# Attention weights turned on VectorE and through DRAM instead of on TensorE, in a fused encoder layer

## The chip, the cores and the metric

The kernel runs on one core of a Trainium2 chip. The metric is the time of one execution on the device, in microseconds (us). Three runs of the kernel before took 1556.53, 1554.85 and 1553.82 us: the median is 1554.85. Five engines run instructions side by side, each in the fixed order of its own queue: TensorE (PE, with its weight load PEld) multiplies matrices and transposes, VectorE (DVE), ScalarE (ACT) and GpSimd (POOL) do elementwise work, and SyncE (SP) issues DMAs. ScalarE issues some DMAs too.

## The reference, cut to what matters

One residual layer of an encoder for 1024 positions (S) of width 1024 (D), all in float32:

```python
h = rmsnorm(x, g_mix)
z = h @ w_in                                  # pooling channels | q | k | v
y_pool = pool_mixer(z[:, :512])               # windows of 2, 4, 8, 16
# per head (8), two maps i (head dimension 64), values of width 128:
s_i = qn_i @ kn_i.T - slope * |dist|          # masked to chunks of 64
a   = softmax(s_0) - lam * softmax(s_1)
o   = head_rmsnorm(a @ v) * 0.8
gates  = sigmoid(h @ w_gate + b_gate)
merged = gates[:, :D] * (y_pool @ w_bp) + gates[:, D:] * (o @ w_ba)
x = x + merged @ w_out
x = x + square(relu(rmsnorm(x, g_ffn) @ w_up)) @ w_down
```

What matters here is `a @ v`: TensorE sums over the partition axis, so it needs `a` with the keys on the partitions, while the scores come out with the queries there. The weights have to be turned in between.

## The kernel before, in words

**Precision.** Every large product is made from float32 operands split into a rounded part hi and a rest lo. `split` (L115) makes hi with a ScalarE cast (L117) and lo with a subtraction on VectorE or GpSimd (L118); `mm3` (L120) issues three products (L123 to L125).

**Stages.** First come input norm, the projections of q, k and v, attention, and beside it the projections for gates and pooling; then the branch projections (tiles bp, ba), the output projection, and the two halves of the MLP. The change touches only the first stage. The 1024 queries are cut into 8 blocks t of 128, so a head has 8 steps and attention has 64 steps g = 8h + t.

**The steps of attention.** `stage` (L620) gives for each letter a generator. A (`stage_qkv`, L418): one z tile of 384 columns, 24 products. B (`stage_prep`, L430): norms of q and k, from a sum of squares (L436, L437), a power on GpSimd (L249) and a product on VectorE (L441); splits v. C (`stage_qkT`, L453): two TensorE transposes of q and k into a PSUM tile tk (L459), then six ScalarE casts and six VectorE subtractions on half tiles of 64 x 128 (L468 to L473) into K and Q. D (`stage_scores`, L477): products of scores, t + 1 key blocks wide (L499, L500), the distance penalty and row minimum on VectorE (L502), the exponential on ScalarE (L510), and the combination of the two maps on VectorE (L519); the result, s, lies with the queries on the partitions. E (`stage_aT`, L545): transposes of each 128 x 128 block of s on TensorE into a PSUM tile ta (L555), up to four at a time, split into AT tiles. F (`stage_pv`, L565), for each pair p of query blocks: 6 (p + 1) products of V with AT, 256 columns wide (tile po). H and R sum squares for the output norm. W loads the next head's weights.

**Order.** A loop over g issues, at step g, the letter with offset n for item g - n; the offsets stand in one string, and offsets between letters say by how many steps a later letter trails. The gate and pool projections are made by `gates` and `pool_group` (L700 to L757), 40 units in all, a unit being 24 products of 512 columns (tiles g and u), their weights loaded on SP (L671) and split on ScalarE and GpSimd. In the text they stand behind the whole of attention. The text's order gives priorities: a scheduler lays each engine's queue out ahead of the run, taking at each moment of its own simulated time the ready instruction that comes first in the text. So the gate units, though last in the text, lie between attention's instructions wherever TensorE would otherwise have stood.

**Buffers.** K (two tiles), V (two), s (one tile for t < 4, two otherwise), AT (1, 2, 3 and 4 tiles for the four pairs) and some early tiles all come from one pool U of eleven buffers of 4 KB per partition; a tile takes a free buffer and gives it back after its last reader. z has two PSUM banks, tk and ta share two, the fillers have one.

```python
O = "B1 C2 H6 D3 R7 E4 F5 W-2 A0"
ORDER = [(w[0], int(w[1:])) for w in O.split()]
N_U, N_W, N_RAW, N_V = 11, 8, 2, 6
```

Of the kernel before, what the change touches and what calls it, by code (L numbers as in the profile page):

```python
# [8 lines left out]
F32 = mybir.dt.float32  # L9
# [25 lines left out]
N_Q, N_QN = 3, 2  # L35
N_Z, N_S, N_T, N_F = 2, 2, 2, 1
N_YU = 5
# [10 lines left out]
O = "B1 C2 H6 D3 R7 E4 F5 W-2 A0"  # L48
ORDER = [(w[0], int(w[1:])) for w in O.split()]
G_FIRST, G_Z = 13, 13  # L50

# [4 lines left out]
def encoder_kernel(  # L56
# [187 lines left out]
    yd = dram.tile([S, D], F32, name="yd")  # L244

# [41 lines left out]


    with ExitStack() as ph:
        sp = ph.enter_context(tc.tile_pool(name="sp", bufs=1))  # L290
        ps_s = ph.enter_context(tc.tile_pool(name="ps_s", bufs=N_S, space=PSUM))
        ps_o = ph.enter_context(tc.tile_pool(name="ps_o", bufs=1, space=PSUM))
        ps_t = ph.enter_context(tc.tile_pool(name="ps_t", bufs=N_T, space=PSUM))

        def s1(shape, dt, name, tag, bufs=1):
            return sp.tile(shape, dt, tag=tag, name=name, bufs=bufs)

        xs = {}

        def utf(shape, name):  # L300
            return ut(shape, F32, name)

        def kv_tiles(h):
            K = [ut([P, 2, 512], F32R, f"K{h}_{i}") for i in range(2)]
            V = [ut([P, 4, 2, P], F32R, f"V{h}_{i}") for i in range(2)]
            KV[h] = (K, V)

        def load_x(t):
            xs[t] = ut([P, D], F32, f"x{t}")
            for c in range(0, D, 512 if t == 0 else D):  # L310
                e = c + 512 if t == 0 else D
                nc.sync.dma_start(xs[t][:, c:e], x[t * P : (t + 1) * P, c:e])

        w_qkv = w_in[:, POOLD:].rearrange("(kk p) (s c) -> p kk s c", p=P, s=3)
        Wh = {}

        raws = {}

        def load_w(h, kp, raw_fn=raw):
            rw = raw_fn([P, 2, 384], f"rqkv{h}_{kp}")  # L320
            for i in range(2):
                nc.sync.dma_start(
                    rw[:, i, :].rearrange("p (s c) -> p s c", s=3),
                    w_qkv[:, 2 * kp + i, :, h * P : (h + 1) * P],
                )
            raws[h, kp] = rw

        def norm_x(t):
            if t % 4 == 0:
                hT.update(alloc_T(htile, "hT", t // 4))  # L330
            if FU >> t & 1:
                hn = fu_tile(f"hn{t}")
            else:
                hn = ut([P, D], F32, f"hn{t}")
            banks = [(ps_t, "tr"), (ps_s, "sc")][: 2 if t < N_SC else 1]
            norm_transpose(xs.pop(t), gmb, t, hT, hn, sp, banks, t == 0)

        def split_w(h, kp, eng):
            rw = raws.pop((h, kp))
            for i in range(2):  # L340
                w = wt([P, 2, 384], f"wqkv{h}_{2 * kp + i}")
                split(w[:, 0, :], w[:, 1, :], rw[:, i, :], eng)
                Wh.setdefault(h, []).append(w)

        KV = {}
        hT = {}
        for w in START.split():
            if w[0] == "x":
                load_x(int(w[1]))
            elif w[0] == "n":  # L350
                norm_x(int(w[1]))
            elif w[0] == "w":
                load_w(0, int(w[1]), utf if w[2:] else raw)
            elif w[0] == "s":
                split_w(0, int(w[1]), nc.gpsimd if w[2:] else nc.vector)
            elif w[0] == "g":
                gmb = ut([P, D], F32, "gmb")
                nc.sync.dma_start(gmb, g_mix[0].partition_broadcast(P))


        rows = sp.tile([32, P], F32, name="rows")
        nc.gpsimd.memset(rows, 0.0)
        nc.sync.dma_start(rows[0:16, :], b_gate[0].rearrange("(r p) -> r p", p=P))
        nc.sync.dma_start(rows[16:20, :], pool_scale[0].rearrange("(r p) -> r p", p=P))
        nc.sync.dma_start(rows[20:21, :], g_sub)

        gqk = sp.tile([P, 2, HD], F32, name="gqk")
        nc.sync.dma_start(gqk[:, 0, :], g_q[0].partition_broadcast(P))
        nc.sync.dma_start(gqk[:, 1, :], g_k[0].partition_broadcast(P))
        lqk = s1([P, 4, HD], F32, "lqk", "oq")  # L370
        nc.sync.dma_start(lqk, lambda_qk[0].partition_broadcast(P))

        dist = sp.tile([P, S], F32, name="dist")

        def distances():

            di = ut([P, S], I32, "di")
            nc.gpsimd.iota(di, pattern=[[-1, S]], base=S - P, channel_multiplier=1)
            nc.scalar.activation(dist, di, AF.Abs)
            nc.gpsimd.memset(dist[0:64, S - 64 : S], MASKED)  # L380

        def columns():
            cols_ps = ps_t.tile([P, 512], F32, tag="tr", name="cols_ps")
            nc.tensor.transpose(cols_ps[:, 0:32], rows, identf[0:32, 0:32])
# [17 lines left out]
        nlam = sp.tile([P, 1], F32, name="nlam")  # L402

        st = {}
        ATs = {}
        Zs = {}
        SS = {}

# [915 lines left out]
```

## Time and profile before

| | |
|---|---|
| median of the three runs | 1554.85 us |
| span of the profiled execution, first to last instruction | 1551.6 us |
| median of the runs above that span | 3.2 us |
| instructions | 22088 |
| TensorE clock granted | 1.000 |
| packets and bytes of DMA | 168009, 206.94 MB |

The profile is of one execution. An engine's busy time is the time in which at least one of its instructions runs; TensorE's instructions overlap, so that the sum of a group's durations and the group's busy time differ. A row of a group gives line, engine, operation, the tiles written and read (buffer numbers left out), the shape, the count, then the busy time in us and the mean duration of one in ns, then the idle time of the engine before these instructions with what ended it. A row of the timeline gives start, duration and the instruction. A row of the waits gives who waited for whom, us in total, times, and the longest. A row of DMA issues gives count, size of one, and the median us from issue to landing. "SPq" is the queue of SyncE.

### The profile page before, as it was taken

The numbers are of one execution on the slowest core, as the hardware profiler recorded it, in microseconds if no ns is written. First come the engines' busy times: TensorE is split into PE (matmuls) and PEld (weight loads), VectorE is DVE, ScalarE is ACT, GpSimd is POOL, SyncE is SP. The second block draws the span as 40 slices with busy tenths as digits, with TensorE's granted clock in tenths as the row PEclk, the third lists the DMA queues.
The fourth block names the chain that finished last, engine by engine and source line by source line (L and its number), as shares of the span: only waits on it lengthen the run. The fifth ranks groups of instructions, "written<-read, shape, count | busy, mean of one in ns | idle before, by whom it ended". The sixth has DMA issues, their size and how long they took to land.

```text
span 1551.6 us, 22088 instructions
## 1 busy us (share of the span) xinstructions
PE 1533.6 (99%) x7649; PEld 1320.8 (85%) x7649; DVE 1011.3 (65%) x2277; ACT 816.7 (53%) x1810; POOL 354.8 (23%) x449
## 2 busy tenths in 40 slices
PE   7999999999999999999999999999999999999999
PEld 6999999999998989888888887888888788888887
DVE  7777677777878787746422458866665667556662
ACT  6656556656566555645532547565555633333331
POOL 5433334243525262324363400000000000000000
PEclk9999999999999999999999999999999999999999
DMA  7111212021202031248536534554343799437650
GB/s 229 51 53 48 66 41 68 24 75 37 75 28 83 28 96 42 69 147 284 179 122 210 168 112 124 182 185 155 129 142 109 278 334 370 170 122 257 224 190 27
DMA packets 168009, 206.94 MB, mean 133 GB/s; under 512 B 10117, under 2 KB 104026, under 8 KB 167898
## 3 DMA queue, kind: packets, MB, share of 16 engines
q1 hardware_dynamic: 150490, 178.23, 35.0%
q10 hardware_dynamic: 17408, 27.30, 4.7%
q8 instruction: 60, 0.98, 0.3%
q14 instruction: 51, 0.42, 0.1%
HBM read 150.94 MB, written 54.56 MB: 132 GB/s over the span
## 4 chain that ended last, share of the span: by engine, by line
PE 89%; DVE 4%; DMA 3%; ACT 1%; issue 1%; POOL 1%; SPq 0%; ACTq 0%; POOLq 0%; DVEq 0%
PE z L125 5%; PE z L123 5%; PE z L124 5%; PE Da L124 4%; PE Da L123 4%; PE Da L125 4%; PE g L123 3%; PE g L124 3%; PE g L125 3%; PE Db L124 3%; PE Db L123 3%; PE Db L125 3%; PE X L125 2%; PE X L123 2%; PE X L124 2%; PE sc L499 2%
## 5 line engine op out<-in xcount | busy, mean ns | idle before, releaser
L123 PE MATMUL z<-wqkv,hT 128*128 128x384 f32 x512 | 174.7, 342 | 0.4 <-DVE qn L441 0.3
L125 PE MATMUL z<-wqkv,hT 128*128 128x384 f32 x512 | 174.3, 341 | 0.5 <-DVE hT L118 0.5
L124 PE MATMUL z<-wqkv,hT 128*128 128x384 f32 x512 | 173.8, 339 | 0.0
L510 ACT ACTIVATE s<-s,nm 128x256 f32<-128x256 f32 (+7 forms) x128 | 99.6, 778 | 49.2 <-DVE nm L502 44.1
L249 POOL TENSOR_TENSOR ms<-ms,mhalf 128x4 f32<-128x4 f32 x64 | 66.6, 1040 | 157.7 <-DVE ms L248 139.1
L125 PE MATMUL g<-hT,fwgate 128*128 128x512 f32 x256 | 101.0, 394 | 0.0
L124 PE MATMUL g<-hT,fwgate 128*128 128x512 f32 x256 | 100.9, 394 | 0.0
L123 PE MATMUL g<-hT,fwgate 128*128 128x512 f32 x256 | 100.9, 395 | 0.0
L123 PEld LDWEIGHTS z<-wqkv,hT 128*128 128x128 f32 x512 | 96.9, 189 | 4.2 <-DVE qn L441 1.0
L125 PEld LDWEIGHTS z<-wqkv,hT 128*128 128x128 f32 x512 | 96.7, 189 | 3.3 <-DVE hT L118 1.3
L124 PEld LDWEIGHTS z<-wqkv,hT 128*128 128x128 f32 x512 | 96.8, 189 | 2.9
L502 DVE CUSTOM_DVE_ANT_0 s<-sc,dist 128x512 f32<-128x512 f32 (+3 forms) x128 | 74.7, 586 | 22.1 <-PE sc L500 20.7
L118 POOL TENSOR_TENSOR wqkv<-rqkv,wqkv 128x384 fp32r<-128x384 f32 x60 | 63.3, 1072 | 17.7 <-ACT wqkv L117 15.3
L499 PE MATMUL sc<-K,Q 128*128 128x512 f32 (+2 forms) x192 | 67.2, 355 | 0.1
L118 DVE TENSOR_TENSOR AS<-s,AS 128x512 fp32r<-128x512 f32 x64 | 43.8, 687 | 35.8 <-ACT AS L117 35.6
L500 PE MATMUL sc<-K,Q 128*128 128x512 f32 (+2 forms) x192 | 66.6, 354 | 0.0
L473 ACT CAST Q<-tk 64x128 fp32r<-64x128 f32 x128 | 33.2, 260 | 58.6 <-DVE Q L472 56.8
L447 POOL TENSOR_TENSOR qn<-qn,ggh 128x128 f32<-128x128 f32 x64 | 32.6, 510 | 137.5 <-DVE qn L441 124.2
L470 ACT CAST Q<-tk 64x128 fp32r<-64x128 f32 x128 | 33.1, 259 | 50.5 <-DVE K L469 49.1
L118 POOL TENSOR_TENSOR fwgate<-frgate,fwgate 128x512 fp32r<-128x512 f32 x32 | 45.2, 1416 | 52.2 <-ACT fwgate L117 52.0
L125 PEld LDWEIGHTS g<-hT,fwgate 128*128 128x128 f32 x256 | 48.1, 188 | 8.6
L123 PEld LDWEIGHTS g<-hT,fwgate 128*128 128x128 f32 x256 | 48.2, 188 | 7.1
(429 smaller groups left out, 4649.6 us busy)
## 6 DMA issues: line engine op xcount, KB each, us to landing
wd<-in_w_down_dram SPq DMA_DIRECT2D x56, 512.0 KB, 5.5
wu<-in_w_up_dram SPq DMA_DIRECT2D x32, 512.0 KB, 5.3
udS<-us SPq DMA_DIRECT2D x64, 256.0 KB, 2.5
ur<-udS SPq DMA_DIRECT2D x32, 512.0 KB, 3.2
rqkv<-in_w_in_dram SPq DMA_DIRECT2D x64, 192.0 KB, 2.8
ud<-u ACTq DMA_DIRECT2D x48, 256.0 KB, 2.2
ur<-ud SPq DMA_DIRECT2D x24, 512.0 KB, 5.5
frgate<-in_w_gate_dram SPq DMA_DIRECT2D x32, 256.0 KB, 2.6
```

Of the source, the lines that this page charges most:

```text
L118: return (lo_eng or nc.vector).tensor_tensor(lo, src, f(hi), op=ALU.subtract)
L123: nc.tensor.matmul(ps, lhs_hi, rhs_hi, start=first, stop=False, **kw)
L124: nc.tensor.matmul(ps, lhs_hi, rhs_lo, start=False, stop=False, **kw)
L125: nc.tensor.matmul(ps, lhs_lo, rhs_hi, start=False, stop=last, **kw)
L249: nc.gpsimd.tensor_tensor(dst, dst, mhalf[:, :n], op=ALU.pow)
L447: nc.gpsimd.tensor_tensor(qn[:, 2:4, :], qn[:, 2:4, :], ggh.unsqueeze(1).broadcast_to([P, 2, HD]), op=ALU.mult)
L470: nc.scalar.copy(q_hi, q)
L473: nc.scalar.copy(Q[other, m, 1, :], q)
L499: nc.tensor.matmul(dst, Q[:, i, 0, :], rhs, start=True, stop=False)
L500: nc.tensor.matmul(dst, Q[:, i, 1, :], rhs, start=False, stop=True)
L502: nc.vector.tensor_tensor_reduce(out=s[i][:, c : c + w], in0=sc[:, 0:w], in1=dist[:, o0 + c : o0 + c + w], scale=2.0 ** -(h + 1), scalar=B ...
L510: nc.scalar.activation(s[i][:, 0:n], s[i][:, 0:n], AF.Exp, bias=last, scale=-1.0, accum_out=Z[:, i, t : t + 1])
```

## The change

The turning of the weights leaves TensorE. A new letter T (`stage_turn`) transposes s on VectorE in one instruction, which turns each block of 32 x 32 in its place, into a tile `turned` of its own, with one buffer. The 32-blocks still have to change places: SP stores `turned` to DRAM in four DMAs, one for each 32 partitions, in runs of 128 (t + 1) bytes, and loads it back in one DMA per group of four key blocks into the lo half of the AT tile, in runs of up to 512 bytes. E then splits in place: a ScalarE cast from SBUF, and a subtraction that moves from VectorE to GpSimd. F reads AT in eight runs of 32 columns.

C takes two query blocks at a time: four transposes into one PSUM tile, then the same six casts and six subtractions on half tiles of 64 x 256. Q has two buffers of double size.

The order is stretched: "B1 C2 H8 D4 T5 R9 E6 F7 W-2 A0", and the loop runs three steps longer. The 40 gate and pool units are issued inside the loop, half a unit a step from step 4 on until 34 are placed, and the rest behind it. The functions that make them are the same and stand further up.

To make room, small tiles of the start share buffers with others (rows, gqk, lqk, gg, lp, rT), the squares of B are written where qn will be, and `ggh` is doubled from head to head. `yt_tile` counts in halves; for the numbers given it picks the same buffers.

```diff
-N_Q, N_QN = 3, 2
+N_Q, N_QN = 2, 3
...
-O = "B1 C2 H6 D3 R7 E4 F5 W-2 A0"
+O = "B1 C2 H8 D4 T5 R9 E6 F7 W-2 A0"
+F_FROM, F_PACE, F_UNITS = 4, 0.5, 34
...
+    turn_dram = {
+        (i, t): dram.tile([4, 32, 4, (t + 1) * 32], F32, name=f"turn{i}_{t}") for i in range(2) for t in range(NT)
+    }
...
     def stage_qkT(h, t):
...
+            for j in range(2):
+                qn = st[h, t + j]["qn"]
+                for i in range(2):
+                    nc.tensor.transpose(
+                        tk[:, i, j, :], qn[:, 2 * i : 2 * i + 2, :].rearrange("p a b -> p (a b)"), identf
+                    )
+            Q = sp.tile([P, 2, 2, 2 * P], F32R, tag="Q", name=f"Q{h}_{t}", bufs=N_Q)
...
-                q, k = tr[own, 0:P], tr[own, P : 2 * P]
+                q, k = tr[own, 0 : 2 * P], tr[own, 2 * P : 4 * P]
...
+        def stage_turn(h, t):
+
+            yield
+            if t % 2 == 0:
+                new_AT(h, t // 2)
+            n = (t + 1) * P
+            a = st.pop((h, t))["a"]
+            turned = sp.tile([P, 4, t + 1, 32], F32, tag="turned", name=f"tn{h}_{t}")
+            nc.vector.transpose(
+                turned.rearrange("p c k q -> p k c q"), a[:, 0:n].rearrange("p (k c q) -> p k c q", c=4, q=32)
+            )
+            room = turn_dram[h % 2, t]
+            for i in range(4):
+                nc.sync.dma_start(
+                    room[:, :, i, :].rearrange("c r x -> r c x"),
+                    turned[32 * i : 32 * (i + 1)].rearrange("r c k q -> r c (k q)"),
+                )
+            for j, (_, lo) in enumerate(ATs[h, t // 2]):
+                nb = min(4, t + 1 - 4 * j)
+                if nb > 0:
+                    nc.sync.dma_start(
+                        f(lo[:, t % 2, :, 0:nb, :]).rearrange("p i k q -> p i (k q)"),
+                        room[:, :, :, 128 * j : 128 * j + 32 * nb].rearrange("c r i x -> (c r) i x"),
+                    )
+            yield
 
         def stage_aT(h, t):
...
-                for i in range(nb):
-                    nc.tensor.transpose(
-                        ta[:, i * P : (i + 1) * P], a[:, (4 * j + i) * P : (4 * j + i + 1) * P], identf
-                    )
...
-                split(hi[:, 0:nb, qc : qc + P], lo[:, 0:nb, qc : qc + P], src)
+                if nb > 0:
+                    hi, lo = (v[:, t % 2, :, 0:nb, :] for v in (hi, lo))
+                    split(hi, lo, f(lo), nc.gpsimd)
+                    yield
...
         def stage_pv(h, p):
...
+                hi, lo = (g[:, :, :, kt % 4, :].rearrange("p t i q -> p (t i) q") for g in groups[kt // 4])
...
-        for g in range(-2, N + 8):
+        units, made = fillers(), 0
+        for g in range(-2, N + 11):
...
+            while made < F_UNITS and made < (g - F_FROM) * F_PACE:
+                next(units)
+                made += 1
+        for _ in units:
+            pass
```

More of the change, by code (lines that the diff above doesn't have):

```diff
@@ L34 @@
 N_FW, N_FR, N_FO = 4, 2, 2
-N_Q, N_QN = 3, 2
+N_Q, N_QN = 2, 3
 N_Z, N_S, N_T, N_F = 2, 2, 2, 1
-N_YU = 5
+N_YU = 10
 N_QKVW = 8 * H
@@ L754, in gates, with fillers @@
             yield
-    gate_units = gates()
-    for _ in range(G_FIRST):
-        next(gate_units)
-    for g in range(4):
-        for _ in pool_group(g):
-            next(gate_units)
-    for _ in gate_units:
-        pass
+    def fillers():
+        gate_units = gates()
+        for _ in range(G_FIRST):
+            next(gate_units)
+            yield
+        for g in range(4):
+            for _ in pool_group(g):
+                yield
+                next(gate_units)
+                yield
+        for _ in gate_units:
+            yield
```

645 lines of the change are left out of this document (317 added, 328 removed).

## Prediction

> **What bounds the kernel now.** I read the page's first two parts, then the windows, then who waits for whom, then the groups of the stage that the change touches. The page says that TensorE has hardly an idle moment:
>
> ```profile
> span 1551.6 us, 22088 instructions
> PE 1533.6 (99%) x7649; PEld 1320.8 (85%) x7649; DVE 1011.3 (65%) x2277; ACT 816.7 (53%) x1810; POOL 354.8 (23%) x449
> ```
>
> The windows answer for the stretch from 60 to 660 us, most of the attention stage (columns: length, then PE, PEld, DVE, ACT, POOL busy, clock, DMA share, GB/s):
>
> ```profile
> 60.00:660.00 600.00, 598.02 (x3451) 549.97 (x3450) 458.34 (x1462) 362.40 (x1052) 226.42 (x311) 1.00 0.18 56
> ```
>
> TensorE is at 598 of 600 us at clock 1.00; VectorE is at 76%, ScalarE at 60%, GpSimd at 38%, the DMA engines at 18%. All of TensorE's waits between 60 and 680 us are these three:
>
> ```profile
> PE ta L555 <- DVE AT_0l L118: 1.0, 1, 1.0
> PE ta L555 <- DVE AT_4l L118: 0.6, 1, 0.6
> PE z L123 <- DVE qn L441: 0.3, 1, 0.3
> ```
>
> So here the end is set by what TensorE issues, and an instruction taken off it counts in full, as long as the others keep up. They do not do so by a wide margin: attention itself is slower than TensorE, and the gate and pool products (tiles g, u) fill its gaps. The step that sets attention's pace is read from the first and last combination of the maps with 512 keys or fewer, and from one head's end:
>
> ```profile
> L519 DVE SCALAR_TENSOR_TENSOR s<-s,cf x32: 350/544/1430, 55.3 to 628.4; 128x128 f32<-128x128 f32 x8, 128x256 f32<-128x256 f32 x8, 128x384 f32<-128x384 f32 x8, 128x512 f32<-128x512 f32 x8
> ```
> ```profile
> 283.77 0.35 DVE L519 SCALAR_TENSOR_TENSOR s<-s,cf 128x128 f32<-128x128 f32 x1
> ```
> ```profile
> 289.07 0.35 POOL L542 MEMSET AT<- 128x128 f32 x2 [0.63 <-PE po L123]
> ```
> ```profile
> 293.66 0.27 PE L555 MATMUL ta<-identf,s 128*128 128x128 f32 x1
> ```
>
> From head 0, block 0 to head 7, block 3 are 59 steps in 573.1 us: 9.7 us a step. Head 3's first weights are ready at 284.1 us, the memset that opens their AT tile runs at 289 once a product of PV has let a buffer go, and they are turned at 293.7. They lie in one of the eleven U buffers for 9.5 us: those buffers pace attention, beside VectorE.
>
> **What goes from TensorE.** The transposes of the weights: 8 heads x 36 blocks = 288. The group row gives a busy time, but a 0.27 us transpose overlaps its neighbour, so I take starts (timeline, TensorE):
>
> ```profile
> L555 PE MATMUL ta<-identf,s 128*128 128x128 f32 x288 | 46.8, 272 | 1.6 <-DVE AT_0l L118 1.0 <-DVE AT_4l L118 0.6
> ```
> ```profile
> 318.44 0.60 PE L555 MATMUL ta<-identf,s 128*128 128x128 f32 x4
> 318.79 0.47 PE L123 MATMUL yp<-mix,wgrp 128*128 128x512 f32 x1
> 319.11 0.39 PE L124 MATMUL yp<-mix,wgrp 128*128 128x512 f32 x1
> 319.33 0.39 PE L125 MATMUL yp<-mix,wgrp 128*128 128x512 f32 x1
> ```
>
> From 318.44 to 319.11 are 0.67 us for four transposes and one 512-wide product, which alone takes 0.22 (319.11 to 319.33). Four cost 0.45, one 0.112: **288 x 0.112 = 32.4 us**. The busy row's 46.8 is the other end. The q and k transposes (tk) stay on TensorE, four to a pair instead of two to a block, the same number.
>
> **PV's operand.** The 480 PV products now read the turned weights in eight runs of 32 columns. No row shows such a run. The nearest is the score product of block 0, which reads one 128-column run twice and lies in the same group as block 1's single run of 256:
>
> ```profile
> L499 PE MATMUL sc<-K,Q 128*128 128x256 f32 x64 | 18.3, 285 | 0.0
> L123 PE MATMUL po<-AT_0h,V 128*128 128x256 f32 x96 | 27.2, 283 | 0.0
> ```
>
> ```profile
> 294.73 0.28 PE L123 MATMUL po<-AT_4h,V 128*128 128x256 f32 x1
> 294.85 0.28 PE L124 MATMUL po<-AT_4l,V 128*128 128x256 f32 x1
> ```
>
> 285 ns against 283: a second run costs nothing, and I take 0 for eight. The upper bound is a rate halved: 0.12 us more for each, the distance between the two starts just shown, 58 us; nothing speaks for a gain.
>
> **VectorE.** It loses the subtractions of E, and halves the count of those of C at double width; it gains 64 block transposes:
>
> ```profile
> L118 DVE TENSOR_TENSOR AT_0l<-ta,AT_0h 128x512 fp32r<-128x512 f32 (+1 forms) x48 | 32.0, 666 | 24.6 <-ACT AT_0h L117 23.1 <-PE sc L500 0.8
> L118 DVE TENSOR_TENSOR AT<-ta,AT 128x128 fp32r<-128x128 f32 (+1 forms) x32 | 11.3, 353 | 4.0 <-ACT AT L117 3.8
> L118 DVE TENSOR_TENSOR AT_4l<-ta,AT_4h 128x384 fp32r<-128x384 f32 (+1 forms) x16 | 9.9, 621 | 1.1 <-ACT AT_4h L117 1.0
> L469 DVE TENSOR_TENSOR K<-tk,K 64x128 fp32r<-64x128 f32 x128 | 37.0, 289 | 16.3 <-ACT K L468 12.4
> L441 DVE TENSOR_TENSOR qn<-z,ms 128x256 f32<-128x256 f32 x64 | 26.8, 418 | 14.4 <-PE tk L459 9.8 <-POOL ms L249 3.4 <-POOL AT_4h L542 1.1
> L519 DVE SCALAR_TENSOR_TENSOR s<-s,cf,s 128x640 f32<-128x640 f32 (+3 forms) x32 | 35.6, 1112 | 0.6
> L519 DVE SCALAR_TENSOR_TENSOR s<-s,cf 128x128 f32<-128x128 f32 (+3 forms) x32 | 19.0, 593 | 0.5
> ```
>
> E: -53.2 us. C: three such groups (L469, L471, L472, all 289 ns), 111.0, become 192 at 256 columns, by the L441 row 0.418: 80.3, so -30.7. A 32x32 block transpose is in no row; the nearest is L519, SBUF to SBUF on the same 64 shapes: 35.6 + 19.0 = +54.6. That is my value; twice it, if four-byte elements go at half rate, is the upper end. Net -29 us, from -53.2 - 30.7 + 54.6; at the upper end +25. ScalarE's six casts of C are merged alike; its 96 casts of E stay, reading SBUF. Neither sets the end, so none of this enters the sum: it decides whether attention can step in 9.7 - 32.4/64 = 9.2 us.
>
> The Trainium skill (VectorE: DVE Perf Modes, "The three transpose paths" and "Rules for kernel authors") speaks against the change: transpose 128x128 on TensorE if PSUM will do, 390 ns there, 311 on VectorE for 32x32 blocks alone, both for bf16. By it 288 blocks would be an estimated 90 us on VectorE and its net would be +6; the trace's 0.112 us is far under its 390.
>
> **GpSimd.** It takes E's 96 subtractions: per head six of 512 columns, two each of 384, 256 and 128.
>
> ```profile
> L118 POOL TENSOR_TENSOR wqkv<-rqkv,wqkv 128x384 fp32r<-128x384 f32 x60 | 63.3, 1072 | 17.7 <-ACT wqkv L117 15.3 <-PE g L125 1.8 <-DMA rqkv<-in_w_in_dram 0.5
> L118 POOL TENSOR_TENSOR fwgate<-frgate,fwgate 128x512 fp32r<-128x512 f32 x32 | 45.2, 1416 | 52.2 <-ACT fwgate L117 52.0
> L118 POOL TENSOR_TENSOR wgrp<-rgrp,wgrp 128x128 fp32r<-128x128 f32 x4 | 1.9, 464 | 1.9 <-ACT wgrp L117 1.9
> ```
>
> 6 x 1.416 + 2 x (1.072 + 0.77 + 0.464) = 13.1 us a head (0.77 midway between its neighbours), 105 in all: 226 + 105 of 600 us, 55%. Hidden while GpSimd has slack; queued behind such a subtraction are the powers (L249) that release z's banks.
>
> **The trip.** Each of 64 blocks issues four stores and one or two loads on SP: 256 + 96 DMAs, 18.9 MB out and in.
>
> ```profile
> 313.52 0.37 SPq L671 DMA_DIRECT2D frpool<-in_w_in_dram  x1
> ```
> ```profile
> L117 ACT CAST AT_0h<-ta 128x512 fp32r<-128x512 f32 (+1 forms) x48 | 27.2, 566 | 7.8 <-PE ta L555 5.8 <-PE sc L500 0.4 <-PE g L125 0.4
> ```
> ```profile
> rqkv<-in_w_in_dram SPq DMA_DIRECT2D x64, 192.0 KB, 2.8
> ...
> y_dram<-oS ACTq DMA_DIRECT2D x32, 128.0 KB, 1.8
> ```
>
> SP: 352 x 0.37 = 130 us of issuing. Block 7: turn 1.3, four issues 1.5, landing 1.8, two issues 0.7, landing 2.8, a ScalarE cast 0.57, subtraction 1.4: 10.1 us, where now transpose 0.45, cast 0.57 and subtraction 0.67 make 1.7. So 8.4 us more; the order puts PV three steps behind the scores instead of two, 9.7 us more. Covered, by little; but the weights' U buffer is free after the turn instead of after the 9.5 us wait above, and DRAM holds them. Loads wait on SP for their stores, and the next weights (frgate, rqkv) queue behind them; the casts wait on ScalarE for the loads, with exponentials and squares behind. For the stalls this leaves on TensorE I estimate 5 us, some three times the 1.9 of the waits above, with 0 and 64 us (1 us a block) as ends.
>
> **Fillers** move no work; they are issued half a unit a step, so that 34 of 40 units are placed by step 71. Cost 0; what is left covers the drain.
>
> **Sum.** 1551.6 - 32.4 + 5 = 1524.2 of span. The median of the runs lies 3.2 us above that span; with it 1527.
>
> **Rivals.**
> (A) Forecast, TensorE stays the bound: 1527, own range 1515 (removal midway to the busy row's end, 39.6 us, and no stall) to 1542 (20 us of stalls). Chance 0.52.
> (B) Attention does not get faster: eleven U buffers and VectorE hold its step near 9.7 us, so the stage ends almost when it did and TensorE idles through the 32 us. For it: VectorE at 76% now, and the 9.5 us wait for a buffer, since AT buffers are held some microseconds longer during the trip; against it: the weights' buffer is freed sooner and VectorE's net is -29. Half to all of the gain lost: 1538 to 1555, middle 1547. Chance 0.24, of which 0.07 within 0.2% (1551.7 to 1558.0; about what a measurement tells from no change). By the Trainium skill's bf16 price above (VectorE: DVE Perf Modes, "The three transpose paths") this case would weigh more.
> (C) Slower: the trip's landings come later than the fixed order allows, ScalarE stands at the casts (L117) with all its queue, and the stall reaches TensorE once a block. It decides from 32.4/64 = 0.51 us a block; at 1 us it is 1527 + 64 = 1591. For it: the cover is 9.7 against 8.4; against: 40% idle time on ScalarE, and no wait of TensorE on a DMA here now. Chance 0.19.
> (D) PV's short runs cost: from 32.4/480 = 0.068 us a product it is slower, at half rate 1527 + 58 = 1585. Chance 0.05.
> Faster 0.52 + 0.17 = 0.69, same 0.07, slower 0.19 + 0.05 = 0.24. The range, 1515 to 1578, leaves out the upper half of C and D and a little below A.
>
> **What would show it.** Right: TensorE's count falls by 288, the span by some 28 us, all before the first bp product; PV still 0.28 us busy; VectorE's transposes near L519's durations; TensorE waits under 10 us in the stage. Wrong: waits of TensorE on AT, K or z summing to tens of us (B, or C if ScalarE's own wait is for the AT loads), PV longer (D), or gaps after the last z.

## The result, and the profile after

| | before | after |
|---|---|---|
| median of four runs | 1554.72 us | 1571.28 us |
| lowest and highest | 1553.82, 1556.53 | 1568.68, 1572.51 |
| span of the profiled execution | 1551.6 | 1566.9 |

The ratio is 1.0105, with a 95% interval of 1.0093 to 1.0117: the changed kernel is slower by 1%, where faster had been forecast. The page of the kernel after has these lines (span; busy time by engine; DMA in all; shares of the chain that ended last, by engine):

```profile
span 1566.9 us, 21985 instructions
...
PE 1520.0 (97%) x7361; PEld 1297.2 (83%) x7361; DVE 988.5 (63%) x2053; ACT 790.5 (50%) x1618; POOL 454.4 (29%) x545
...
DMA packets 249420, 244.72 MB, mean 156 GB/s; under 512 B 48517, under 2 KB 184410, under 8 KB 249306
...
PE 70%; DMA 11%; DVE 9%; ACT 4%; issue 3%; SPq 2%; POOL 1%; DVEq 0%; ACTq 0%; POOLq 0%
```

TensorE has 7649 - 7361 = 288 instructions less, as the change says, and is still 97% busy. But the chain now runs through transfers for 11% of the span and through VectorE for 9%; the same line of the kernel before reads 89% PE, 4% DVE and 3% DMA. TensorE no longer sets the end all by itself. The window of 60 to 660 us, for the kernel after:

```profile
60.00:660.00 600.00, 577.40 (x3155) 520.82 (x3154) 436.09 (x1253) 338.30 (x872) 317.19 (x403) 0.99 0.42 114
```

TensorE does nothing for 22.6 of 600 us, where it was 2.0. VectorE and ScalarE have become emptier, not fuller (436 against 458, 338 against 362); GpSimd is at 53%; the DMA engines' share went from 0.18 to 0.42.

Where does the stage end? The first branch product, tile bp, follows on the last projection. The rows of that tile give durations, then first and last start; first the kernel before, then after:

```profile
L123 PE MATMUL bp<-ypT,wbp x64: 389/389/500, 701.0 to 744.4; 128*128 128x512 f32 x64
```
```profile
L124 PE MATMUL bp<-ypT,wbp x64: 389/389/395, 715.5 to 758.5; 128*128 128x512 f32 x64
```

From there to the end of the span it is 850.6 us before and 851.4 after: all but 0.8 us of the difference arose before the first bp, which comes 14.5 us late. If the 288 transposes were worth their 32.4 us, some 47 us were lost in the same stage. ScalarE's waits for the loads of turned weights between 60 and 660 us in the kernel after (who waited for whom, us in total, times, longest):

```profile
ACT AT_0h L118 <- DMA AT_0l<-turn: 54.2, 27, 5.5
ACT AT L118 <- DMA AT<-turn: 35.9, 16, 4.5
...
ACT AT_4h L118 <- DMA AT_4l<-turn: 9.3, 9, 4.6
```

ScalarE stood before 52 of its 96 casts, 99.4 us in all. How that reaches TensorE is seen from head 2's block 5, in the timeline of the kernel after (start, duration, instruction; "SPq" is SyncE's queue):

```profile
256.71 0.97 DVE L664 STREAM_TRANSPOSE tn<-s 128x768 f32<-128x768 f32 x1
...
257.70 1.76 SPq L669 DMA_DIRECT2D turn<-tn  x4
...
260.11 0.35 ACT L580 CAST K<-tk 64x256 fp32r<-64x256 f32 x1
...
262.70 0.53 SPq L676 DMA_DIRECT2D AT_0l<-turn  x1
...
265.94 0.62 ACT L118 CAST AT_0h<-AT_0l 128x512 fp32r<-128x512 f32 x1 [5.48 <-DMA AT_0l<-turn]
...
266.46 0.36 ACT L582 CAST Q<-tk 64x256 fp32r<-64x256 f32 x1
...
266.86 0.42 DVE L583 TENSOR_TENSOR Q<-tk,Q 64x256 fp32r<-64x256 f32 x1 [3.96 <-ACT Q L582]
...
271.94 0.69 DVE L615 CUSTOM_DVE_ANT_0 s<-sc,dist 128x512 f32<-128x512 f32 x1
```
```profile
272.69 0.50 PE L612 MATMUL sc<-K,Q 128*128 128x512 f32 x1 [2.59 <-DVE nm L615]
```

The block is turned by 257.68. The four stores are issued by 259.46; the loads wait in SyncE's queue until these have landed, and go at 262.70 (over the whole run this queue waits 96 times for such stores, 93.1 us in all); the first load lands 3.2 us later. ScalarE came to the cast at 260.46, 2.8 us after the turn, and stood there until 265.94. Behind that cast, in the same queue, lay the casts of the next q and k pair (Q, L582), whose PSUM tile the cast into K had read at 260.11 already. VectorE waited 3.96 us for them, then had a backlog that put the next score reduction (L615) at 271.94, and TensorE, which needed the score bank that this reduction frees, stood for 2.59 us. None of TensorE's waits in this run is put down to a transfer: here it waits for VectorE, which waited for ScalarE, which waited for the load.

This block is one of the worst. The timelines of VectorE and ScalarE give the same two times for all 64 blocks. ScalarE comes to the first of a block's casts 1.7 to 9.4 us after the end of its turn, with a median of 5.6. The 48 first casts that had to wait start at a median of 7.0 us after it. So ScalarE is typically a microsecond or two too early, and in the block shown 5.5.

### The profile page after: what moved, and what is told of

It reads as the page before. It is cut to its first block, busy times and chain, and to the rows that moved or that the text cites. A ratio compares the mean times of both kernels' runs of the same rounds, so it can differ in the third digit from the quotient of the medians.

```text
span 1566.9 us, 21985 instructions
## 1 busy us (share of the span) xinstructions
PE 1520.0 (97%) x7361; PEld 1297.2 (83%) x7361; DVE 988.5 (63%) x2053; ACT 790.5 (50%) x1618; POOL 454.4 (29%) x545
## 2 busy tenths in 40 slices
DMA packets 249420, 244.72 MB, mean 156 GB/s; under 512 B 48517, under 2 KB 184410, under 8 KB 249306
## 4 chain that ended last, share of the span: by engine, by line
PE 70%; DMA 11%; DVE 9%; ACT 4%; issue 3%; SPq 2%; POOL 1%; DVEq 0%; ACTq 0%; POOLq 0%
PE Da L125 4%; PE Da L124 4%; PE Da L126 4%; DMA turn<-tn 3%; PE Db L125 3%; PE Db L124 3%; PE Db L126 3%; DMA AT_0l<-turn 3%; PE z L126 3%; PE z L125 3%; PE X L126 2%; PE X L124 2%; PE z L124 2%; PE X L125 2%; PE ba L126 2%
## 5 line engine op out<-in xcount | busy, mean ns | idle before, releaser
L119 POOL TENSOR_TENSOR AT_0l<-AT_0l,AT_0h 128x512 fp32r<-128x512 f32 (+1 forms) x48 | 62.1, 1293 | 75.8 <-ACT AT_0h L118 74.9
L615 DVE CUSTOM_DVE_ANT_0 s<-sc,dist 128x512 f32<-128x512 f32 (+3 forms) x128 | 74.1, 584 | 14.6 <-PE sc L613 12.6
L118 ACT CAST AT_0h<-AT_0l 128x512 fp32r<-128x512 f32 (+1 forms) x48 | 28.9, 602 | 70.5 <-DMA AT_0l<-turn 69.7
L124 PEld LDWEIGHTS g<-hT,fwgate 128*128 128x128 f32 x256 | 48.7, 190 | 14.8 <-ACT yps L363 2.7
L126 PEld LDWEIGHTS g<-hT,fwgate 128*128 128x128 f32 x256 | 48.7, 190 | 11.1 <-POOL fwgate L119 1.1
L125 PEld LDWEIGHTS g<-hT,fwgate 128*128 128x128 f32 x256 | 48.8, 191 | 9.0
L664 DVE STREAM_TRANSPOSE tn<-s 128x128 f32<-128x128 f32 (+3 forms) x64 | 49.4, 773 | 8.2 <-DMA turn<-tn 7.4
```

The source lines that it names most:

```text
L118: nc.scalar.copy(hi, src)
L119: return (lo_eng or nc.vector).tensor_tensor(lo, src, f(hi), op=ALU.subtract)
L124: nc.tensor.matmul(ps, lhs_hi, rhs_hi, start=first, stop=False, **kw)
L125: nc.tensor.matmul(ps, lhs_hi, rhs_lo, start=False, stop=False, **kw)
L126: nc.tensor.matmul(ps, lhs_lo, rhs_hi, start=False, stop=last, **kw)
L615: nc.vector.tensor_tensor_reduce(out=s[i][:, c : c + w], in0=sc[:, 0:w], in1=dist[:, o0 + c : o0 + c + w], scale=2.0 ** -(h + 1), scalar=B ...
```

## The experiments

The theory (number 1 in the expectations): the trip through DRAM is longer than the queues of the engines have been laid out for, ScalarE stands at its casts until a load has landed, and its other work, K, Q and the exponentials, comes late to VectorE and TensorE. The rivals: the even issue of the projections costs (2); the pairs of C and the stretched order hold K, V and q longer (3); the subtractions on GpSimd come late (4); the AT tiles, held during the trip, keep the U buffers (5). Every time is the median of the runs; the ratio is to the kernel before, run beside it (medians of 1554.0 to 1555.3 us), with its interval in brackets. "First bp" is the start of the first branch product, "waits" what ScalarE waited for the AT loads between 60 and 660 us.

| run | time | ratio to before | first bp | waits |
|---|---|---|---|---|
| before | 1554.7 | | 701.0 | none |
| e1_pairs | 1570.3 | 1.0107 [1.0090, 1.0124] | 717.4 | none |
| e2_even | 1555.8 | 1.0010 [1.0001, 1.0020] | 703.2 | none |
| e3_noturn | 1555.0 | 1.0005 [0.9996, 1.0014] | 702.7 | none |
| e5_notrip | 1525.9 | 0.9812 [0.9798, 0.9827] | 671.6 | none |
| e14_later_held2 | 1531.0 | 0.9846 [0.9832, 0.9861] | 677.6 | 4.4 |
| e11_heldsub | 1540.9 | 0.9912 [0.9892, 0.9931] | 684.1 | 60.3 |
| e6_held | 1541.4 | 0.9914 [0.9899, 0.9930] | 687.3 | 61.9 |
| e8_noland | 1543.1 | 0.9925 [0.9906, 0.9943] | 689.5 | 89.5 |
| e13_later_held1 | 1543.1 | 0.9924 [0.9907, 0.9940] | 692.8 | 62.7 |
| e10_later | 1545.6 | 0.9946 [0.9926, 0.9966] | 693.3 | 77.9 |
| e7_dvesub | 1561.4 | 1.0045 [1.0025, 1.0064] | 706.7 | 92.0 |
| e9_own | 1563.1 | 1.0055 [1.0040, 1.0070] | 708.6 | 98.2 |
| after | 1571.3 | 1.0105 [1.0093, 1.0117] | 715.5 | 99.4 |
| e12_double | 1593.8 | 1.0254 [1.0239, 1.0269] | 742.1 | 119.9 |
| e4_behind | 1609.7 | 1.0360 [1.0345, 1.0376] | 757.3 | 96.2 |

### The parts of the change

**Paired C alone, in the kernel before** (the order stretched by the step that a pair needs, nothing else):

```diff
-N_Q, N_QN = 3, 2
+N_Q, N_QN = 2, 3
-O = "B1 C2 H6 D3 R7 E4 F5 W-2 A0"
+O = "B1 C2 H7 D4 R8 E5 F6 W-2 A0"
...
-            elif w == "C":
-                yield from stage_qkT(h, t)
+            elif w == "C" and t % 2:
+                yield from stage_qkT(h, t - 1)
```

> The kernel before with one part of the change: C takes two query blocks at a time, with the order stretched by the one step that this needs (D4, E5, F6), weights still turned on TensorE, gate and pool units still behind attention in the text. Theory 1 (the DRAM trip: ScalarE stands at the casts until a load has landed, and what is queued behind it comes late to TensorE): pairs are harmless, TensorE has the same work, so 1550 to 1556 us. Theory 2 (the even issue of gate and pool units): the same. Theory 3 (pairs and the stretched order hold K, V and q longer): slower, 1560 us or more.

1570.3 us, and no trip in it. The windows of this run show where:

```profile
540.00:600.00 60.00, 57.99 (x340) 51.42 (x338) 48.23 (x146) 37.13 (x99) 18.82 (x31) 1.00 0.15 49
600.00:660.00 60.00, 52.67 (x246) 41.92 (x244) 31.89 (x75) 22.36 (x45) 16.94 (x21) 0.94 0.23 76
660.00:720.00 60.00, 58.12 (x254) 47.19 (x253) 6.59 (x10) 18.33 (x30) 13.61 (x11) 1.00 0.44 143
```

Attention got faster: its last score product starts at 618.9 us instead of 668.3. But the gate projections go on to 717, with little beside them, and TensorE idles 11.2 us of the 180; 6.5 of these it waits until ScalarE has read out the bank of a finished product (go, u, yps). The middle row's clock of 0.94 is one stretch of 6.8 us at half clock. VectorE is at 6.59 of 60 in the last row. A faster attention is no gain when the work that filled its gaps is left over. The time is what theory 3 had expected (1560 or more), and not theory 1; whether the pairs are the cause of the change's loss, the third run below decides.

**The even issue alone**, in the kernel before (the functions moved up, the loop as in the diff of the change):

```diff
+F_FROM, F_PACE, F_UNITS = 4, 0.5, 34
...
+            while made < F_UNITS and made < (g - F_FROM) * F_PACE:
+                next(units)
+                made += 1
```

> The kernel before with another part alone: gate and pool units issued half a unit a step inside the loop, the rest unchanged. Theory 1: no change, 1552 to 1558 us. Theory 2 (units issued in the loop go ahead of attention's later steps, attention gets slower and TensorE is left without spare work where attention stalls): slower by 10 us or more, 1565 us or more. Theory 3: no change.

1555.8 us: no more than 0.2% from no change. There was nothing to smooth.

**The change without the turn**: the kernel after, with the weights turned by TensorE as before (order as in the first experiment), C paired and the projections evenly issued.

```diff
-O = "B1 C2 H8 D4 T5 R9 E6 F7 W-2 A0"
+O = "B1 C2 H7 D4 R8 E5 F6 W-2 A0"
...
+                ta = ps_t.tile([P, 512], F32, tag="tr", name=f"ta{h}_{t}_{j}")
+                for i in range(nb):
+                    nc.tensor.transpose(
+                        ta[:, i * P : (i + 1) * P], a[:, (4 * j + i) * P : (4 * j + i + 1) * P], identf
+                    )
...
+                split(hi[:, 0:nb, qc : qc + P], lo[:, 0:nb, qc : qc + P], src)
```

> The changed kernel with the turning put back on TensorE (E transposes and splits as before, order D4, E5, F6), pairs and even issue kept: the change without the trip. Theory 1: all of the loss is gone, 1548 to 1556 us, and TensorE's waits in the stage fall from about 47 us to under 10. Theories 2 and 3: the loss stays and the transposes come on top, 1580 us or more.

1555.0 us: the time of the kernel before. The even issue gives back the 15 us that pairing costs. Theory 3 falls, which expected 1580 or more here. Whatever made the change 17 us slower lies in the turn.

**The change without the even issue**: all 40 units behind the loop.

```diff
-F_FROM, F_PACE, F_UNITS = 4, 0.5, 34
+F_FROM, F_PACE, F_UNITS = 4, 0.5, 0
```

> The changed kernel with the gate and pool units issued behind the loop again, as before, so that they only fill gaps. Theory 1: TensorE still stands when ScalarE does; at most the units fill some of it, 1560 to 1572 us. Theory 2: the gain of the removed transposes comes out, 1525 to 1540 us. Theory 3: 1565 us or more.

1609.7 us, so theory 2 falls: the even issue saves 38 us. Theory 1 had not foreseen it either; its 1560 to 1572 took the fillers' order as harmless. ScalarE waits no longer than after (96 us), but TensorE more. Its two longest waits between 60 and 757 us here:

```profile
PE sc L612 <- DVE nm L615: 18.8, 14, 4.4
PE g L124 <- ACT go L371: 5.3, 4, 3.5
```

In the kernel after the first of them is 6.2 us. Up to the first bp TensorE idles 65.7 us here (757.3 less 691.6 busy) against 39.3 there (715.5 less 676.2). And the last score product starts at 628.4 us, 44 earlier than after, but from it to the first bp it is 129 us instead of 43: as with the pairs alone, attention draws ahead, and the projections that could have covered its stalls are made behind it, alone.

### The trip

**No trip.** Stores and loads are gone, and E splits straight from `turned`. This leaves out the exchange of the 32-blocks, so the output isn't the reference's; every other instruction is there.

```diff
-                    split(hi, lo, f(lo), nc.gpsimd)
+                    split(hi, lo, turneds[h, t][:, :, 4 * j : 4 * j + nb, :], nc.gpsimd)
```

> The changed kernel without stores and loads: E's cast and subtraction read the tile of the block transposes directly, all else kept (block transposes, GpSimd's subtractions, PV in eight runs, pairs, even issue). Left out: the exchange of the 32x32 blocks between partitions. Theory 1 (the trip is what loses the time): TensorE's stalls fall from 57 us in the first 780 us to about 12, as in the variant with the turning on TensorE, and the 32 us of transposes come out: 1520 to 1532 us. Theory 4 (GpSimd's 96 subtractions hold up the powers that release z): little changes, 1560 to 1572 us. Theory 5 (the U buffers are held longer while the trip runs): as theory 1.

1525.9 us. Its first bp product, and its rows for VectorE's transposes and a PV product in the window 60 to 660 us:

```profile
L124 PE MATMUL bp<-ypT,wbp x64: 389/389/389, 671.6 to 714.5; 128*128 128x512 f32 x64
```
```profile
L665 DVE STREAM_TRANSPOSE tn<-s 128x128 f32<-128x128 f32 (+3 forms) x64 | 49.3, 770 | 0.9
```
```profile
L124 PE MATMUL po<-AT_0h,V 128*128 128x256 f32 x96 | 27.2, 283 | 0.0
```

Transposes, short runs, GpSimd's subtractions, paired C, even issue, the stretched order: together they give all of the forecast's gain. What was lost, 715.5 - 671.6 = 43.9 us up to the first bp, is the trip's. How it divides is told by one window each, from the start to the first bp, first the kernel after, then this one:

```profile
0.00:715.50 715.50, 676.18 (x3649) 606.50 (x3650) 497.60 (x1403) 395.12 (x1003) 365.70 (x476) 0.99 0.44 123
```
```profile
0.00:671.60 671.60, 658.73 (x3649) 602.93 (x3650) 513.51 (x1403) 394.55 (x1002) 365.32 (x475) 1.00 0.23 74
```

The same 3649 products on TensorE: 26.4 us of the 43.9 are more idle time (39.3 against 12.9), and 17.5 are products that take longer. Three stretches of 3.4 us at half clock (last section) account for at most 5.1 of these; the rest was not traced, and would come from products that no longer overlap their neighbours.

**The wait doubled.** Each store is issued twice, the same data to the same place.

```diff
-                nc.sync.dma_start(
-                    room[:, :, i, :].rearrange("c r x -> r c x"),
+                for _ in range(2):
+                    nc.sync.dma_start(
+                        room[:, :, i, :].rearrange("c r x -> r c x"),
```

> The changed kernel with each of its 256 stores of turned weights issued twice, the same data to the same place. That lengthens the trip by four more issues on SP (1.5 us) and some share of a second landing (up to 2 us), and adds 9.4 MB of traffic. Theory 1: without a trip 1526, with it 1571, so 45 us for some 8 us of trip beyond what was there; 1.5 to 3.5 us more a block, with the order's cover used up, come to TensorE for the most part: 64 blocks, 40 to 200 us, so 1610 us or more, with ScalarE's waits for AT loads growing by about as much. If the trip's length is not what counts (theories 4 and 5), 1571 to 1585 us.

1593.8 us: 22.5 more than after, and ScalarE's waits 20.5 more. The expectation of 1610 was too high, and the second issue added 18.9 MB (263.63 against 244.72), not 9.4. The direction, and that the waits grow by about as much as the time, is theory 1's, and the other two gave at most 1585.

**Loads that need not wait for their stores' landing.** They read the room that the head before has written, opened by a small GpSimd copy from `turned`; so from the second head on other data are used than the reference's.

```diff
+            old = turn_dram[(h + 1) % 2, t] if h else room
...
+                    nc.gpsimd.tensor_copy(lo[:, t % 2, 0, 0, 0:2], turned[:, 0, 0, 0:2])
...
-                        room[:, :, :, 128 * j : 128 * j + 32 * nb].rearrange("c r i x -> (c r) i x"),
+                        old[:, :, :, 128 * j : 128 * j + 32 * nb].rearrange("c r i x -> (c r) i x"),
```

> The changed kernel with the loads no longer waiting for the stores of the same block: they read the room that the head before wrote (left out: the right data from head 1 on), and a GpSimd copy of two columns from the turned tile into AT in front of each load keeps them behind the block transpose (96 small GpSimd instructions more). Traffic and number of DMAs stay. Theory 1, in the form that the trip's length counts: some 3 to 4 us shorter a block, ScalarE's waits fall by a third or more and the time to 1545 to 1565 us. In the form that the wait of ScalarE is only the error between the landing that the fixed order assumes and the real one: half of the error goes, about the same time. If DMA traffic by itself is what costs: no change, 1568 to 1575 us.

1543.1 us: with the landing of the stores out of the trip, 28 us come back. But ScalarE's waits are still 89.5 us, hardly below the 99.4, where a third less had been expected. The timelines show part of the reason: the first casts start 6.1 us after the turn instead of 7.0, but ScalarE also comes to them sooner, after 5.1 instead of 5.6 (medians). So the sum of its waits isn't the price. It may matter what stands behind each cast and how late that already is; what decides it here was not traced further.

**The subtractions back on VectorE.**

```diff
-                    split(hi, lo, f(lo), nc.gpsimd)
+                    split(hi, lo, f(lo))
```

> The changed kernel with E's 96 subtractions back on VectorE. Theory 4 (GpSimd): most of the loss is gone, 1535 to 1555 us. Theory 1: the casts still wait for the loads, and VectorE stands behind them too, 1568 to 1590 us.

1561.4 us, 10 less than after, and between what the two theories expected. Either GpSimd's queue is a cost (theory 4), or the trip's end merely comes earlier: a subtraction of 512 columns (AT_0l) takes 0.77 us on VectorE here, 1.35 on GpSimd in the kernel after. The run e11 below tells.

### Where the casts stand

**Casts held behind the next block's exponential.** An edge of order on ScalarE, no wait on another engine: E's casts are laid behind the last exponential of the block that follows.

```diff
+        exps = {}
...
-                nc.scalar.activation(
+                exps[h, t] = nc.scalar.activation(
...
-                    split(hi, lo, f(lo), nc.gpsimd)
+                    nxt = exps.get(divmod(h * NT + t + 1, NT))
+                    with ExitStack() as held:
+                        if nxt is not None:
+                            held.enter_context(tc.issue_after(nxt.ins))
+                        split(hi, lo, f(lo), nc.gpsimd)
```

> The changed kernel with one edge more in ScalarE's order, no wait: the casts of E for a block stand behind the last exponential of the next block, so that ScalarE does not reach them before the load has landed. Theory 1, in the form that ScalarE's standing (99 us of waits for the loads between 60 and 660 us) is what reaches TensorE: ScalarE's waits for loads fall below 30 us and the time to 1535 to 1555 us. Theory 5 (buffers, not ScalarE's order): AT tiles are held still longer, so no gain or slower, 1570 us or more. Theory 4: no change.

1541.4 us, 30 less than after and faster than before, by the same work in another order (21986 instructions against 21985). ScalarE's waits for AT loads are 61.9 us, more than the 30 expected: ScalarE now comes to a block's first cast 6.7 us after the turn (median), still short of the 7.0 of the landing in the kernel after.

**The control**: the same edge, to the block's own exponential, which has run long before.

```diff
-                    nxt = exps.get(divmod(h * NT + t + 1, NT))
+                    nxt = exps.get(divmod(h * NT + t, NT))
```

> The control for the held casts: the same extra edge, but each block's ScalarE casts stand behind the exponential of their own block, which has run long before. If holding gained because the casts moved in ScalarE's queue (theory 1: ScalarE stands at a cast until its load has landed and its queue comes late to TensorE), this stays at the changed kernel's 1571 us, within 4 us, and ScalarE's waits for AT loads between 60 and 660 us stay near 99 us. If the edge by itself does something (any other reason), it goes towards the 1541 us of the held casts.

1563.1 us: waits as after (98.2) and casts at the same place (5.5 us after the turn), but 8 us faster than after, which the expectation denied. The edge alone changes how the queues are laid out, in a way that was not followed up. What the place of the casts is worth is then 1563.1 - 1541.4 = 21.7 us, not 30.

**Held casts and subtractions on VectorE together.**

> The held casts with E's 96 subtractions on VectorE instead of GpSimd. Alone, the move of the subtractions gained 10 us over the changed kernel (1561 against 1571). If that gain was a shorter trip (theory 1: the end of the trip comes 0.7 us earlier a block), the held casts cover it already and this gives 1538 to 1543 us. If GpSimd's queue is a cost of its own (theory 4: subtractions late behind others on GpSimd), the gain adds: 1530 to 1534 us.

1540.9 us: nothing is added to the 1541.4 of the held casts. That is what was expected if the 10 us of the subtractions were trip length. Theory 4 falls, also by the run without a trip, which has all its subtractions on GpSimd and 1525.9 us.

**The later order**: E, F, H and R one step later in the string, nothing held.

```diff
-O = "B1 C2 H8 D4 T5 R9 E6 F7 W-2 A0"
+O = "B1 C2 H9 D4 T5 R10 E7 F8 W-2 A0"
...
-        for g in range(-2, N + 11):
+        for g in range(-2, N + 12):
```

> The changed kernel with E, F, H and R one step later in the order string (H9 R10 E7 F8, one more turn of the loop); nothing else. Theory 1 (the trip is longer than the order covers, and ScalarE stands at the casts): a step more, 9.7 us, covers the trip, ScalarE's waits for AT loads fall well under 99 us and the time comes to 1530 to 1550 us. Theory 5 (what is lost is lost to the U buffers that AT tiles hold during the trip): AT is held a step longer, so 1571 us or more, with VectorE and ScalarE waiting for PV to release buffers. In between, both.

1545.6 us. By the order the AT tiles lie a step longer in the U buffers, and the kernel is 26 us faster: theory 5 falls. The waits fall less than expected, to 77.9 us: one more order step, 9.7 us, brings ScalarE to the first cast only 0.9 us later (6.5 after the turn).

**Both: later order and held casts**, first behind the next block's exponential, then behind that of the block after it (t + 2 in the line of e6_held).

> The later order (E, F, H, R one step later, 1545.6 us alone) and each block's casts held behind the exponential of the next block (1541.4 us alone, and 1563 with the edge put where it holds nothing). One step later, the next block's exponential is an earlier step's: the edge asks for little that the order does not ask already. If holding and the later order return the same thing, the place of the casts in ScalarE's queue behind the landing, this gives 1536 to 1546 us. If they are two things that add (26 and 22 us), about 1526 us, the time without a trip.

> The later order with the casts held behind the exponential of the block after next, so that both the text's order and ScalarE's queue have the casts a full step further from their load than in the held casts alone. If what is left of the loss (1541 against 1526) is still the trip and ScalarE's wait for it, ScalarE's waits for AT loads between 60 and 660 us fall under 30 us and the time to 1526 to 1535 us. If what is left is the price of the AT tiles that lie in the U buffers longer, or of the DMA traffic, it stays at 1538 us or rises.

The first gives 1543.1: with the order a step later, that edge asks for little that the order doesn't ask, and nothing adds. The second gives 1531.0 us. All of ScalarE's waits for AT loads, and the window, in this kernel between 60 and 660 us:

```profile
ACT AT_4h L118 <- DMA AT_4l<-turn: 3.2, 3, 1.4
ACT AT_0h L118 <- DMA AT_0l<-turn: 1.2, 1, 1.2
```
```profile
60.00:660.00 600.00, 596.10 (x3298) 545.84 (x3297) 459.64 (x1279) 350.09 (x899) 339.58 (x415) 1.00 0.46 123
```

4.4 us of waits instead of 99.4, TensorE at 596 of 600 instead of 577, first bp at 677.6. ScalarE now comes to the first cast 15.4 us after the turn (median). The transfers are all still there (249420 packets, a share of 0.46): traffic as such costs at most the 5 us between this run and the one without a trip. So the cause is shown: it was where the casts stood in ScalarE's queue against the landing of their loads. This run moves PV along with the casts; the pair e6_held and e9_own leaves the order string alone and moves only the casts. This version beats both kernels, by 1.5% and 2.6%.

## Why the prediction was wrong, point by point

- **What goes from TensorE, 32.4 us: right.** The change without the turn and the change without the trip have their first bp at 702.7 and 671.6: 31.1 us for 288 transposes, 0.108 each. TensorE idles about as long in both (13.2 and 12.9 us), so nearly all of the difference is its own work; they also differ in the order's steps, in PV's runs and in the engine of the subtractions. The busy row's 46.8 was far off. The window of the change without the turn:

```profile
0.00:702.70 702.70, 689.46 (x3938) 631.97 (x3939) 487.95 (x1435) 395.06 (x1004) 266.58 (x379) 1.00 0.23 71
```

- **PV's operand, 0: right.** Eight runs of 32 columns: 283 ns in the group above, and 27.2 us of busy time for 96, as before. Rival D is out.
- **VectorE: right in size.** 49.4 us for the 64 transposes after, against 54.6 by L519's rows; the merged subtractions of C took 0.422 each, against 0.418. Rival B, that attention gets no faster, is out: without the trip it stepped fast enough for the whole gain, with the trip and the latest casts (e14_later_held2) for nearly all of it, and with C paired alone it even ran ahead of its fillers.
- **GpSimd: right.** The groups of the kernel after:

```profile
L119 POOL TENSOR_TENSOR AT_0l<-AT_0l,AT_0h 128x512 fp32r<-128x512 f32 (+1 forms) x48 | 62.1, 1293 | 75.8 <-ACT AT_0h L118 74.9 <-PE g L126 0.8
...
L119 POOL TENSOR_TENSOR AT<-AT 128x128 fp32r<-128x128 f32 (+1 forms) x32 | 20.5, 641 | 55.4 <-ACT AT L118 52.1 <-PE z L126 3.3
L119 POOL TENSOR_TENSOR AT_4l<-AT_4l,AT_4h 128x384 fp32r<-128x384 f32 (+1 forms) x16 | 19.8, 1237 | 9.0 <-ACT AT_4h L118 8.9
```

102.4 us in all against 105, and the last column shows GpSimd waiting for ScalarE's casts, not the other way round.

- **The trip's length: about right.** Issues and landings were put at 1.5 + 1.8 + 0.7 + 2.8 = 6.8 us between the turn and the first cast; the median is 7.0, and head 2's block 5, a slow one, took 8.3.
- **The cover, and with it the 5 us of stalls: the step that failed.** The prediction took one order step, 9.7 us, as cover for a trip 8.4 us longer, called it covered, and put the stalls at three times the waits of the kernel before; no row bore on the factor. But an order step is the distance of PV from its scores in the text. The cast is not at PV: it lies in ScalarE's queue, which the scheduler lays out ahead of the run. There it lay a median of 5.6 us behind the turn, less than 9.7 in each of the 64 blocks, and 2.8 in the block shown; a further order step (e10_later) added 0.9, not 9.7. The landing needed 7.0. What stands behind the cast waits with it, in the block shown the next pair's Q. So 5 us became 43.9, or 0.69 us a block: above the 0.51 from which rival C decides. C's mechanism is what happened, with its line (the casts, L118 after) and its queue; it had a chance of 0.19, because ScalarE was 40% idle. Idle time doesn't help an engine that works through its queue in order and stands at one instruction for up to 5.5 us. (C's 1591 us adds its 64 us to a sum that already holds 5; without these it is 1586.)
- **Where the stall shows: half right.** "ScalarE's own wait for the AT loads" was named as the sign of C, and is there; but TensorE's own waits are spread, and nearly all put down to VectorE or ScalarE. The longest sums in the kernel after, 60 to 700 us:

```profile
PE po L124 <- ACT AT_0h L118: 8.5, 5, 4.9
PE sc L612 <- DVE nm L615: 6.2, 7, 2.6
PE g L124 <- ACT yps L363: 2.4, 1, 2.4
```

From these three alone one would put some 17 us down to the trip, not 43.9.
- **Fillers, 0: right in the sum, by luck.** The even issue gives nothing to the kernel before, 15 us back beside the pairs, and 38 us beside the trip. The prediction had no term for the 15 us that the pairs cost; the even issue happened to return them.
- **Sum.** 1524.2 of span with 5 us of stalls; with the measured 43.9 in place of the 5 it is 1563.1, and the measured span is 1566.9. Of the other 3.8 us, 1.3 are the transposes (31.1, not 32.4), 1.7 the pairs and fillers (first bp at 702.7 against 701.0), and 0.8 lie behind the first bp. The range to 1578 held the time, but only because it had been drawn wide enough for half of C; the sign was missed.

What stays open: the 8 us that the edge of the control gains, why e8_noland gains 28 us with waits that hardly fell, and the last 6 us between 677.6 and 671.6. One thing was not tried: `turned` has a single buffer, and VectorE stood five times, 7.4 us in all, until its stores had landed (1.9 us in e14_later_held2).

## What to carry to other kernels

When work is sent on a trip through DMA, cover is not counted in steps of the program but in the queue of the engine that picks the data up: ask how long after the issue that engine gets to the instruction, and what stands behind it. Two experiments cost little and bound everything: the kernel without the trip (what the rest of the change is worth), and the picking up held back by an edge of order (what the place is worth). And work that only fills gaps is part of a stall's price: the same change came out 17 us slower than the kernel before with fillers at an even pace, and 56 with the fillers behind.

## What the runs showed of the hardware

**The clock after a gap.** In the kernel after, TensorE's granted clock was halved for about 3.4 us at each of its three idle times above 2 us in the attention stage (2.59, 2.36 and 4.88 us), and at none of its three of 1.3 to 1.6 us. Here are three windows of it, the first ending with the last product before the gap of 2.59 us shown above (columns as for the windows; the clock is the third from the end):

```profile
264.00:270.00 6.00, 6.00 (x32) 4.93 (x31) 2.60 (x7) 3.99 (x10) 1.98 (x2) 1.00 0.25 66
273.10:276.50 3.40, 3.40 (x14) 3.11 (x13) 2.30 (x7) 2.91 (x7) 1.73 (x3) 0.50 0.77 211
277.00:283.00 6.00, 6.00 (x41) 5.96 (x40) 3.50 (x8) 3.55 (x10) 2.54 (x3) 1.00 0.66 183
```

The PV products in the slow window start 0.21 us apart, in the timeline of the kernel after, against the 0.12 of the two that the prediction quotes:

```profile
273.38 0.41 PE L124 MATMUL po<-AT,V 128*128 128x256 f32 x1
273.59 0.42 PE L125 MATMUL po<-AT,V 128*128 128x256 f32 x1
```

So by estimate the stall of 2.59 us costs up to 1.7 us more (half of 3.4). The same is seen from 631.5 and from 696.3 us on. How long a gap must be is not to be had from these runs: in e8_noland one of 1.93 us was followed by half clock (614.9 to 618.3 us); in e4_behind one of 2.85 us, which ended at 500.2, was not, and other slow stretches of that run lasted 6.8 us. The Trainium skill (TensorE: Matmul & The Clock Gate, "Part 1: The HAM clock gate") gives the half clock after an idle window of some 3.4 us, with windows that run freely; the length of the slow stretch agrees, but here gaps of 2.36 and 2.59 us were enough.

**VectorE's block transpose.** 770 ns on the average of the 64 shapes in float32, 0.97 us at 768 columns and 1.11 at 896, near the rate of the pass that combines the maps. The rule of the Trainium skill (VectorE: DVE Perf Modes, "Rules for kernel authors") to transpose 128 x 128 on TensorE is answered by e14_later_held2: with the weights turned off TensorE it is 1.5% faster than the kernel before, and than the change with the turn on TensorE (1555.0 us), once the trip is covered. With the trip uncovered the rule holds here, by 1%.
